# Attention's modulation products dealt out over three projections, shift columns formed later, and a gating accumulator with the tokens innermost

## The chip, the cores and the metric

The kernel runs on one core of one Trainium2 chip. The metric is the device time of one execution in microseconds. Before the change it is 1385.32 us, the median of three runs (1384.69 to 1388.82).

## The reference

Two transformer blocks follow each other on 256 tokens of 1024 channels, all in float32. Both are steered by a conditioning vector: `mod = silu(c) @ ada_w + ada_b` gives six vectors of 1024, a shift, a scale and a gate for each half of the block. What matters here, shortened:

```python
# block 1
sh1, sc1, g1, sh2, sc2, g2 = split(silu(c) @ ada_w + ada_b, 6)
z  = modulate(rms_norm(x), sh1, sc1) @ w_in + b_in      # mLSTM q k v o i f, attention q k v, gates ga gb
ym = mlstm(...) ; ya = attention(rope(q), rope(k), v)   # 256 keys, causal
merged = sigmoid(ga) * (ym @ p_mlstm) + sigmoid(gb) * (ya @ p_moba)
x  = x + g1 * (merged @ w_out)
h  = modulate(rms_norm(x), sh2, sc2)                    # h * (1 + scale) + shift
x  = x + g2 * ((silu(h @ w_gate) * (h @ w_up)) @ w_down)
# block 2: pooling and SSD mixer, then PEER: 8 heads x 16 of 16384 one-neuron experts
act = gelu(h . expert_down[idx]) ; y = sum(gates * act * expert_up[idx])
```

The expert part is computed densely. All 16384 products of a token with `expert_down` are formed and passed through gelu. They are multiplied by a gating matrix that is zero except at a token's 128 chosen experts, and then multiplied with all of `expert_up`.

## The kernel before, in words

Tokens lie along the free dimension and channels along the 128 partitions. Each weight slab is 128 x 1024 float32, 512 KB. The helper `prep` loads it with a DMA from the SP queue (line 210) and splits it into a high part (`hi`, ScalarE, line 213) and a remainder (`lo`, VectorE, line 218). The activations are split in the same way, and each product is made of three matmuls (`mm3`, lines 275 to 279). `prep` runs at most two slabs ahead; there are three buffers each for `hi` and `lo`. TensorE writes into eight PSUM banks: three of the pool `pp` for projections, five of the pool `sp` for everything else.

A modulation vector is not made by TensorE. A column of 128 values is one product on VectorE: `do_ada` (line 228) multiplies a 128 x 1024 slab of `ada_w` by the row `silu(c)` and sums along the row (line 232); a second small instruction reads the accumulator. Eight such products make one of the six vectors, and after the eighth the bias is added (line 240).

The order of the slabs is a list, `items` (lines 156 to 192). `w_items` puts the slabs of one projection on the list, and the products it is given behind particular slabs: `mix` is spread evenly from slab `lo` to the end, `at` names the slabs. `nxt` takes the next weight slab and first runs the products listed ahead of it (`ada_run`). In the first block the projections come in this order: eight double slabs `wst` for the mLSTM, then `win` with 28 slabs (0 to 7 attention's q and k, 8 to 11 its v, 12 to 27 the two gates ga and gb), `pmo` with 8 (merge), `wout` with 8 (output), `wgu` with 44 and `wdn` with 22 (feed-forward).

Work that isn't a projection is written as generators and advanced by `tick` between projections: the mLSTM (lines 555 to 625) during q and k, attention (`moba`, lines 662 to 721) during the gates. Attention's scores are lines 676 and 679 into `sp` banks; VectorE takes row maxima (683, 684); ScalarE takes exponentials and row sums (688); VectorE normalizes (699); TensorE transposes (708 to 710) and multiplies with v. From gate 9 on, the gate projections leave PSUM through a sigmoid (line 752), which needs another table on ScalarE; that table is loaded (lines 94 and 746) after all exponentials before it.

The text's order is not the engines' order. The context is built with `schedule_with_timeline_sim=True`, and each engine's order is fixed when the program is built. In the trace many instructions stand earlier or later than in the text: gate projections run ahead of the attention scores, whose text comes between them.

`residual` (lines 350 to 385) closes a half block, three times in the kernel: for `wout`, for `wdn` and for the second block's `wout2`. For each of eight blocks of 128 channels it runs the projection, adds the gated result to `xT` (366), and stores the scaled `xT` split into `dH` and `dL` (367, 368), with a running sum of squares. The next projection starts before the normalization is known; so `dH` and `dL` have two more columns that hold the shift, formed ahead of the loop (354 to 356), and the projection of a column is scaled and shifted afterwards.

The gating matrix is built in `gstage` (lines 1226 to 1249) for half of the experts at a time, in 32 groups of eight tokens: `gstage(0)` while `expert_down` is multiplied (`dblock`, from 797 us), `gstage(1)` during the first half of `expert_up` (from 1014 us; `umm`, line 1361). A group has one-hot tiles A and B on VectorE (1232 to 1240), 16 matmuls of 64 columns in float16 (1244), which put the eight tokens' 64 columns side by side in one PSUM bank, and a multiplication of the bank into `W` (1248). `W` is stored expert by expert with the 256 tokens innermost, so this multiplication steps through it with the expert innermost, 1 KB from element to element. `wsplit` (1251 to 1267) splits four experts' columns of `W` into high and low part for the expert sum.

Of the kernel before, what the change touches and what calls it, by code (L numbers as in the profile page):

```python
# [9 lines left out]
F32 = mybir.dt.float32  # L10
# [5 lines left out]
AF = mybir.ActivationFunctionType  # L16
OP = mybir.AluOpType
# [3 lines left out]
T = 256  # L21
# [8 lines left out]
GSC = 32768.0  # L30
# [31 lines left out]
def two_block_kernel(ctx, tc, I, out, dbg=None):  # L62
    nc = tc.nc
    V, S, G, PE = nc.vector, nc.scalar, nc.gpsimd, nc.tensor
# [47 lines left out]
    def pp():  # L112
        return ppool.tile([P, 512], F32, name="pp")

    def sp():
        return spool.tile([P, 512], F32, name="sp")
# [41 lines left out]
    def ada_list(w, ms, kind="g"):  # L158
        return [(kind[(i * KD + k) % len(kind)], I["ada%d" % w][m, k], (w, m, k)) for i, m in enumerate(ms) for k in range(KD)]

    def w_items(name, n, mix=(), lo=0, at=None):
        at = at or {}
        for j, a in enumerate(mix):
            at.setdefault(lo + (j * (n - lo)) // len(mix), []).append(a)
        for i in range(n):
            items.append(("w", I[name][i], None))
            items.extend(at.get(i, []))
# [10 lines left out]
        items.append(("w", I["wst"][k], None))  # L178
        items.append(("w", I["wst"][8 + k], None))
    items.append(("c", None, None))  # L180
    attn = ada_list(1, [2, 3, 4], "d")
    w_items("win", 28, attn[:22], 11)
    w_items("pmo", 8, attn[22:])
    w_items("wout", 8)
    ffn = ada_list(1, [5], "d") + [("c", None, None)] + ada_list(2, [0, 1, 2, 3, 4], "d")
    w_items("wgu", 44, ffn[3:30], 12, {6: ffn[:1], 8: ffn[1:2], 10: ffn[2:3]})
    w_items("wdn", 22, ffn[30:])
# [83 lines left out]
    def mcol(w, m, k):  # L271
        o = (w - 1) * 48 + m * 8 + k
        return mod[:, o:o + 1]
# [23 lines left out]
    def paced(ins, to="lo"):  # L297
        after(ins, cur[to])
        return ins
# [24 lines left out]
    def square(src, scale=None):  # L324
        sq = smallp.tile([P, T], F32, name="sq", bufs=3)
        if scale is None:
            S.activation(sq, src, AF.Square)
        else:
            S.activation(sq, src, AF.Square, scale=scale)
        return sq  # L330
# [19 lines left out]
    def residual(emit, w, m, gi, wsh, msh, dH, dL, scale=None, plain=False, post=None, wait=2):  # L350
        acc = smallp.tile([P, T], F32, name="acc", bufs=1)
        accp = smallp.tile([P, T], F32, name="accp", bufs=1) if plain else None
        o_ = sp()
        sh = mod[:, (wsh - 1) * 48 + msh * 8:][:, :8].unsqueeze(2).to_broadcast([P, KD, 2])
        S.activation(dH[:, :, T:], sh, AF.Copy)
        V.tensor_tensor(dL[:, :, T:], sh, dH[:, :, T:].bitcast(F32), OP.subtract)
        for e in range(8):
            ps = cur["ob"][e] if e in cur.get("ob", {}) else sp() if post is not None and e in (3, 4) else pp()
            emit(ps, e)
            g = gs[:, gi, e:e + 1]  # L360
            src = ps[:, :T]
            if post is not None:
                src = smallp.tile([P, T], F32, name="mt", bufs=3)
                V.tensor_tensor(src, ps[:, :T], post, OP.mult)
                V.tensor_tensor(src, src, ps[:, T:], OP.add)
            V.scalar_tensor_tensor(xT[:, e], src, mcol(w, m, e), xT[:, e], OP.mult, OP.add)
            S.activation(dH[:, e, :T], xT[:, e], AF.Copy, scale=g)
            V.scalar_tensor_tensor(dL[:, e, :T], xT[:, e], g, dH[:, e, :T].bitcast(F32), OP.mult, OP.subtract)
            sq = square(xT[:, e], None if scale is None else scale[:, e:e + 1])
            if e == 0:  # L370
                V.tensor_copy(acc, sq)
            elif e < 7:
                V.tensor_tensor(acc, acc, sq, OP.add)
            else:
                PE.matmul(o_[:, :T], ones, acc, start=True, stop=False)
                lag["mm"] = PE.matmul(o_[:, :T], ones, sq, start=False, stop=True)
                lag["wait"] = wait
            if plain:
                sq = square(xT[:, e])
                if e == 0:  # L380
                    V.tensor_copy(accp, sq)
                else:
                    V.tensor_tensor(accp, accp, sq, OP.add)
        cur["h"] = (dH, dL, TE)
        return o_, accp
# [10 lines left out]
    with p1:  # L396
# [245 lines left out]
        for i in range(8):  # L642
            ps = pp()
# [99 lines left out]
        for n in range(16):  # L743
# [5 lines left out]
            ps = pp()  # L749
# [15 lines left out]
        for e in range(8):  # L765
            ps = pp()
# [15 lines left out]
        flush()  # L782
        make_gs(1, 1, 4, "n2")
        o2, _ = residual(lambda ps, e: proj(ps), 1, 2, 1, 1, 3, hH, hL)
        r2 = rstd_of(o2[:, :T], D, "rstd")

    silu_set()
    with ExitStack() as p2:
# [15 lines left out]
        def prescaled(ps, rstd, name, pool):  # L804
            t = pool.tile([P, T], F32, name=name)
            c = pool.tile([P, 1], F32, name=name + "c")
            V.tensor_copy(c, ps[:, T:T + 1])
            V.tensor_tensor(t, ps[:, :T], rstd, OP.mult)
            return t, c

        for f in range(NF):
# [6 lines left out]
            if f < 4:  # L818
                t, c = prescaled(pg, r2, "tg", w2)
                act(s_, t, AF.Silu, bias=c)  # L820
                t, c = prescaled(pu, r2, "tu", w2)
# [35 lines left out]
    with ExitStack() as p3:  # L857
# [147 lines left out]
        pv = q3.tile([P, 4, T], F32, name="pv")  # L1005
# [15 lines left out]
        for g in range(2):  # L1021
            ps = sp()
# [23 lines left out]
        for i in range(8):  # L1046
            ps = pp()
# [48 lines left out]
    W = [wp.tile([P, 64, T], F32, name="W0"), None]  # L1096
# [11 lines left out]
    with ExitStack() as p4:  # L1108
# [86 lines left out]
        for i in range(16):  # L1195
            ps = pp()
# [29 lines left out]
    GT = 8  # L1226

    def gstage(hf):
        for g0 in range(0, T, GT):
            tsl = slice(g0, g0 + GT)  # L1230
            A = q5.tile([P, GT, 64, 2], F16, name="A")
            paced(V.tensor_tensor(A, iob.rearrange("p (n d) -> p n d", d=2)[:, None].to_broadcast([P, GT, 64, 2]),
                                  i1d[:, tsl, None, :].to_broadcast([P, GT, 64, 2]), OP.is_equal))
            yield
            B = q5.tile([P, 2, GT, 32, 2], F16, name="B")
            V.tensor_tensor(B[:, 0], iob[:, hf * 64:hf * 64 + 64].rearrange("p (n d) -> p n d", d=2)[:, None]
                            .to_broadcast([P, GT, 32, 2]), i2d[:, tsl, None, :].to_broadcast([P, GT, 32, 2]), OP.is_equal)
            for j in (1, 0):
                V.tensor_tensor(B[:, j], B[:, 0], gd[j][:, tsl, None, :].to_broadcast([P, GT, 32, 2]), OP.mult)
            yield  # L1240
            ps = pp()
            for t in range(GT):
                for j in range(2):
                    PE.matmul(ps[:, t * 64:(t + 1) * 64], A[:, t].rearrange("p n d -> p (n d)"),  # L1244
                              B[:, j, t].rearrange("p n d -> p (n d)"), start=(j == 0), stop=(j == 1))
            yield
            wv = W[hf][:, :, tsl].rearrange("p n t -> p t n")
            V.scalar_tensor_tensor(wv, ps.rearrange("p (t n) -> p t n", t=GT), 1.0 / GSC, wv, OP.mult, OP.mult)  # L1248
            yield

    def wsplit(n2):
# [314 lines left out]
```

## Time and profile before

| | |
|---|---|
| median of three runs | 1385.32 us |
| the profiled execution | 1386.68 us |
| its span, first to last instruction | 1384.9 us |
| mean granted TensorE clock | 0.993 |
| TensorE busy | 1355.2 us, 98% |
| VectorE busy | 1163.3 us, 84% |
| ScalarE busy | 715.2 us, 52% |
| SP queue | 283.64 MB, 59.1% of 16 DMA engines |

The profile is that of one execution. PE is TensorE's matmuls, PEld its weight loads, DVE is VectorE, ACT is ScalarE, POOL is GpSimd, SP the queue that issues the DMAs. A row by stretch gives, for each engine, its busy time and the count of its instructions in the stretch; then the clock that TensorE was granted as a share of full speed, the DMA engines' share and GB/s. In a row of the waits, the arrow points to what ended the wait. In a timeline row the bracket holds the idle time of the engine ahead of it and what ended it. Rows that follow each other with the same shape are merged, and xN counts them. Matmuls overlap in the pipeline, so their durations are longer than their spacing.

### The profile page before, as it was taken

How to read it: one execution, taken by the hardware profiler on the slowest of the kernel's cores; microseconds unless marked ns; L12 is line 12 of the kernel's file. 1: busy time of each engine (PE TensorE's matmuls, PEld its weight loads, DVE VectorE, ACT ScalarE, POOL GpSimd, SP SyncE). 2: the span in 40 equal slices, each digit the busy share in tenths (PEclk: the TensorE clock that was granted, in tenths of full speed). 3: DMA queues.
4: the chain of work that ended last, by engine and by line, in shares of the span. 5: the costliest groups of instructions: out<-in, count | busy, mean ns of one | idle time of the engine just before them, and what ended most of it. 6: DMA issues, size and time to landing. Idle time of an engine off the chain costs nothing. (4 is left out here: it accounts for less than half of the span.)

```text
span 1384.9 us, 25895 instructions
## 1 busy us (share of the span) xinstructions
PE 1355.2 (98%) x10306; PEld 1254.4 (91%) x10306; DVE 1163.3 (84%) x2015; ACT 715.2 (52%) x1078; POOL 45.9 (3%) x39
## 2 busy tenths in 40 slices
PE   8999899999999999999999999999999999899997
PEld 6998699999999989999999999999978888788886
DVE  7999867988898798788988888888699999776556
ACT  4564665554546946555545544444544444445444
POOL 0000000000000000122222000000000000000000
PEclk9999899999999999999999999999999999999999
DMA  9968645799995435555555544444455555566563
GB/s 339 345 218 298 228 145 176 239 354 346 328 336 207 150 126 173 175 182 183 182 177 170 189 163 161 169 165 168 168 182 178 173 168 170 179 220 221 203 221 107
DMA packets 79196, 286.78 MB, mean 207 GB/s; under 512 B 8817, under 2 KB 9217, under 8 KB 78946
## 3 DMA queue, kind: packets, MB, share of 16 engines
q1 hardware_dynamic: 78770, 283.64, 59.1%
q8 instruction: 81, 1.33, 0.4%
q0 software_dynamic: 304, 1.47, 0.3%
q14 instruction: 41, 0.34, 0.1%
HBM read 284.03 MB, written 1.05 MB: 206 GB/s over the span
## 5 line engine op out<-in xcount | busy, mean ns | idle before, releaser
L213 ACT ACTIVATE hi<-raw 128x1024 fp32r<-128x1024 f32 x382 | 404.9, 1061 | 503.8 <-PE pp L277 236.5
L218 DVE TENSOR_TENSOR lo<-raw,hi 128x1024 fp32r<-128x1024 f32 x366 | 446.4, 1221 | 113.8 <-ACT hi L213 112.9
L278 PE MATMUL pp<-nH,lo 128*128 128x256 f32 x1064 | 300.2, 284 | 2.5 <-DVE lo L218 2.4
L276 PE MATMUL pp<-nH,hi 128*128 128x256 f32 x1064 | 300.3, 284 | 0.3 <-ACT qT L1204 0.3
L277 PE MATMUL pp<-nL,hi 128*128 128x256 f32 x1064 | 300.3, 283 | 0.0
L1361 PE MATMUL sp<-hi,wHL 128*128 128x512 f32 x992 | 257.3, 396 | 3.5 <-ACT wHL L1262 3.5
L276 PE MATMUL pp<-hH,hi 128*128 128x256 f32 (+1 forms) x824 | 236.6, 287 | 0.0
L278 PE MATMUL pp<-hH,lo 128*128 128x256 f32 (+1 forms) x824 | 232.8, 284 | 0.0
L277 PE MATMUL pp<-hL,hi 128*128 128x256 f32 (+1 forms) x824 | 232.8, 283 | 0.0
L1361 PEld LDWEIGHTS sp<-hi,wHL 128*128 128x128 f32 x992 | 185.6, 189 | 44.4 <-ACT wHL L1262 3.9
L278 PEld LDWEIGHTS pp<-nH,lo 128*128 128x128 f32 x1064 | 200.5, 189 | 3.1 <-DVE lo L218 3.1
L276 PEld LDWEIGHTS pp<-nH,hi 128*128 128x128 f32 x1064 | 200.4, 189 | 0.7 <-ACT qT L1204 0.5
L277 PEld LDWEIGHTS pp<-nL,hi 128*128 128x128 f32 x1064 | 200.7, 189 | 0.2
L277 PEld LDWEIGHTS pp<-hL,hi 128*128 128x128 f32 x824 | 156.4, 190 | 1.2 <-issue 1.1
L276 PEld LDWEIGHTS pp<-hH,hi 128*128 128x128 f32 x824 | 156.3, 190 | 0.8 <-issue 0.5
L278 PEld LDWEIGHTS pp<-hH,lo 128*128 128x128 f32 x824 | 156.1, 190 | 0.8 <-issue 0.7
L1361 PE MATMUL sp<-lo,wHL 128*128 128x512 f32 x496 | 136.6, 393 | 0.0
L1361 PEld LDWEIGHTS sp<-lo,wHL 128*128 128x128 f32 x496 | 93.3, 188 | 20.8
L1248 DVE SCALAR_TENSOR_TENSOR W<-pp,W 128x512 f32<-128x512 f32 x64 | 85.3, 1333 | 23.2 <-PE pp L1244 23.2
L213 ACT ACTIVATE hi<-ada 128x1024 fp32r<-128x1024 f32 x52 | 55.2, 1062 | 58.1 <-PE pp L277 29.3
L232 DVE SCALAR_TENSOR_TENSOR raw<-raw,crow 128x1024 f32<-128x1024 f32 x56 | 68.2, 1219 | 5.3 <-DMA raw<-in_ada 5.2
L218 DVE TENSOR_TENSOR lo<-ada,hi 128x1024 fp32r<-128x1024 f32 x52 | 63.5, 1222 | 7.5 <-ACT hi L213 7.0
(464 smaller groups left out, 1984.2 us busy)
## 6 DMA issues: line engine op xcount, KB each, us to landing
raw<-in_edn SPq DMA_DIRECT2D x128, 512.0 KB, 3.3
raw<-in_eup SPq DMA_DIRECT2D x128, 512.0 KB, 4.0
raw<-in_ada SPq DMA_DIRECT2D x64, 512.0 KB, 5.2
raw<-in_win SPq DMA_DIRECT2D x35, 512.0 KB, 4.5
ada<-in_ada SPq DMA_DIRECT2D x32, 512.0 KB, 5.3
raw<-in_wgu SPq DMA_DIRECT2D x32, 512.0 KB, 5.1
ada<-in_win SPq DMA_DIRECT2D x17, 512.0 KB, 4.7
raw<-in_wq SPq DMA_DIRECT2D x15, 512.0 KB, 3.5
```

Of the source, the lines that this page charges most:

```text
L213: cur["hi"] = S.activation(hi, raw, AF.Copy)
L218: cur["lo"] = V.tensor_tensor(lo, raw, hi.bitcast(F32), OP.subtract)
L232: V.scalar_tensor_tensor(raw, raw, 1.0, cur["crow%d" % w], OP.mult, OP.mult, accum_out=mod[:, o:o + 1])
L276: m = PE.matmul(ps, lh, rh, start=start, stop=False)
L277: PE.matmul(ps, lh, rl, start=False, stop=False)
L278: PE.matmul(ps, ll, rh, start=False, stop=stop)
L1248: V.scalar_tensor_tensor(wv, ps.rearrange("p (t n) -> p t n", t=GT), 1.0 / GSC, wv, OP.mult, OP.mult)
L1361: m = PE.matmul(oacc[q], l[:, a * P:(a + 1) * P], u[:, b], start=n2 == 0 and i == 0, stop=n2 == 127 and i == 2, skip_group_check=True)
```

## The change

Three edits.

1. The 24 products for the vectors 2 (gate g1), 3 (shift sh2) and 4 (scale sc2) change their order and their places. Before: 22 spread over `win` slabs 11 to 27, two in `pmo`, none in `wout`. After: the vectors come in the order 2, 4, 3; three products follow `win` slabs 5, 7 and 9, thirteen are spread over slabs 11 to 27, three stand in `pmo`, and the last five, all of the shift, behind the first five slabs of `wout`.
2. `residual` forms the shift columns ahead of the seventh block (`e == 6`) in place of ahead of the loop, in all three uses.
3. `gstage` writes its matmuls' results with the token innermost: the 64 columns of token t go to every eighth element of the bank, from t on. The multiplication then reads the bank in storage order and steps through `W` in runs of eight tokens.

```diff
@@ the list of slabs
-    attn = ada_list(1, [2, 3, 4], "d")
-    w_items("win", 28, attn[:22], 11)
-    w_items("pmo", 8, attn[22:])
-    w_items("wout", 8)
+    attn = ada_list(1, [2, 4, 3], "d")
+    w_items("win", 28, attn[3:16], 11, {5: attn[:1], 7: attn[1:2], 9: attn[2:3]})
+    w_items("pmo", 8, attn[16:19])
+    w_items("wout", 8, (), 0, {j: attn[19 + j:20 + j] for j in range(5)})
@@ residual
-        S.activation(dH[:, :, T:], sh, AF.Copy)
-        V.tensor_tensor(dL[:, :, T:], sh, dH[:, :, T:].bitcast(F32), OP.subtract)
         for e in range(8):
+            if e == 6:
+                S.activation(dH[:, :, T:], sh, AF.Copy)
+                V.tensor_tensor(dL[:, :, T:], sh, dH[:, :, T:].bitcast(F32), OP.subtract)
@@ gstage
             ps = pp()
+            pv = ps.rearrange("p (n t) -> p n t", t=GT)
             for t in range(GT):
                 for j in range(2):
-                    PE.matmul(ps[:, t * 64:(t + 1) * 64], A[:, t].rearrange("p n d -> p (n d)"),
+                    PE.matmul(pv[:, :, t], A[:, t].rearrange("p n d -> p (n d)"),
                               B[:, j, t].rearrange("p n d -> p (n d)"), start=(j == 0), stop=(j == 1))
             yield
-            wv = W[hf][:, :, tsl].rearrange("p n t -> p t n")
-            V.scalar_tensor_tensor(wv, ps.rearrange("p (t n) -> p t n", t=GT), 1.0 / GSC, wv, OP.mult, OP.mult)
+            wv = W[hf][:, :, tsl]
+            V.scalar_tensor_tensor(wv, pv, 1.0 / GSC, wv, OP.mult, OP.mult)
             yield
```

## Rows read from the trace of the kernel before

**Rows 1.** The page, part 1: busy us (share) xinstructions of each engine.

```profile
PE 1355.2 (98%) x10306; PEld 1254.4 (91%) x10306; DVE 1163.3 (84%) x2015; ACT 715.2 (52%) x1078; POOL 45.9 (3%) x39
```

**Rows 2.** By stretch, end of the input projection: length, busy us (count), clock, DMA.

```profile
156.70:161.20 4.50, 0.42 (x2) 0.19 (x1) 4.50 (x12) 1.02 (x4) 0.00 (x0) 0.88 0.58 223
161.20:168.60 7.40, 5.05 (x15) 3.65 (x16) 2.76 (x14) 6.47 (x29) 0.00 (x0) 0.50 0.39 143
168.60:173.60 5.00, 4.99 (x24) 4.98 (x25) 5.00 (x20) 4.99 (x14) 0.00 (x0) 0.50 0.00 0
173.60:190.00 16.40, 16.40 (x140) 14.65 (x140) 8.51 (x15) 12.43 (x24) 0.00 (x0) 0.99 0.34 107
```

**Rows 3.** Waits of TensorE after 96 us: total us, times, longest us.

```profile
PE sp L676 <- DVE ada L232: 4.1, 1, 4.1
PE sp L1361 <- ACT wHL L1262: 3.5, 1, 3.5
...
PE sp L708 <- DVE P L699: 2.3, 1, 2.3
```

**Rows 4.** VectorE's instructions in order: start us, us, line, operation, tiles, shapes.

```profile
149.05 0.69 DVE L640 TENSOR_TENSOR ro<-ro,rot 128x512 f32<-128x512 f32 x1
...
156.04 1.28 DVE L683 TENSOR_REDUCE nm<-sp 128x2 f32<-128x512 f32 x2
157.24 1.22 DVE L232 SCALAR_TENSOR_TENSOR raw<-raw,crow 128x1024 f32<-128x1024 f32 x1
...
159.98 1.22 DVE L232 SCALAR_TENSOR_TENSOR ada<-ada,crow 128x1024 f32<-128x1024 f32 x1
```

**Rows 5.** ScalarE's instructions in order, the softmax.

```profile
160.17 0.47 ACT L107 ACTIVATE P<-sp,nm 128x256 f32<-128x256 f32 x1 [5.46 <-DVE nm L684]
...
167.87 1.28 ACT L94 ACT_TABLE_LOAD   x1
```

**Rows 6.** By stretch, input to output projection.

```profile
55.00:88.00 33.00, 33.00 (x260) 31.70 (x259) 28.60 (x54) 24.38 (x47) 0.00 (x0) 1.00 0.66 248
88.00:161.00 73.00, 69.12 (x466) 59.64 (x464) 68.88 (x107) 36.49 (x59) 0.00 (x0) 0.99 0.82 294
161.00:215.00 54.00, 51.44 (x387) 48.29 (x388) 36.46 (x80) 36.01 (x86) 0.00 (x0) 0.88 0.39 137
215.00:240.00 25.00, 24.56 (x202) 24.23 (x201) 18.61 (x33) 15.35 (x28) 0.00 (x0) 1.00 0.51 169
```

**Rows 7.** Line 232 from 88 to 161 us: count, then duration ns min/median/max.

```profile
L232 DVE SCALAR_TENSOR_TENSOR raw<-raw,crow x14: 1214/1216/1219, 90.7 to 157.2; 128x1024 f32<-128x1024 f32 x14
...
L232 DVE SCALAR_TENSOR_TENSOR ada<-ada,crow x9: 1214/1217/1220, 88.5 to 160.0; 128x1024 f32<-128x1024 f32 x9
```

**Rows 8.** By stretch, VectorE at line 232 alone.

```profile
88.00:161.00 73.00, 27.87 (x45) 0.99 0.82 294
```

**Rows 9.** By stretch, the second gating half, before its last multiplications.

```profile
1000.00:1188.00 188.00, 188.00 (x1228) 152.36 (x1227) 177.80 (x235) 80.05 (x77) 0.00 (x0) 1.00 0.52 174
```

**Rows 10.** VectorE's instructions in order, the last gating multiplication.

```profile
1191.21 1.15 DVE L1248 SCALAR_TENSOR_TENSOR W<-pp,W 128x512 f32<-128x512 f32 x1
```

**Rows 11.** ScalarE's instructions in order, start of the second half.

```profile
1191.83 1.06 ACT L107 ACTIVATE W<-W 128x1024 f32<-128x1024 f32 x1 [1.92 <-DMA W<-in_cr]
...
1192.99 1.99 ACT L1262 ACTIVATE wHL<-W 128x1024 fp32r<-128x1024 f32 x2
```

**Rows 12.** TensorE's instructions in order, start of the second half.

```profile
1194.09 3.57 PE L1361 MATMUL sp<-hi,wHL 128*128 128x512 f32 x8 [3.52 <-ACT wHL L1262]
...
1198.52 1.98 PE L1361 MATMUL sp<-hi,wHL 128*128 128x512 f32 x8
```

**Rows 13.** The page, part 5: xcount | busy us, mean ns | idle.

```profile
L1248 DVE SCALAR_TENSOR_TENSOR W<-pp,W 128x512 f32<-128x512 f32 x64 | 85.3, 1333 | 23.2 <-PE pp L1244 23.2
```

**Rows 14.** Groups of VectorE by line, 120 to 160 us.

```profile
L639 DVE TENSOR_TENSOR rot<-sp,sin_t 128x512 f32<-128x512 f32 x3 | 2.1, 684 | 1.5 <-PE sp L636 1.5
```

**Rows 15.** By stretch, TensorE at line 1244 alone.

```profile
1188.92:1189.87 0.95, 0.95 (x32) 0.95 (x32) 1.00 1.06 392
```

## The prediction

> **What bounds the kernel now.** I read the engine line of the page first. TensorE is busy 1355.2 of 1384.9 us [rows 1], so a change that adds no matmul can win back only TensorE's idle time and the time it runs at a low clock. The views by stretch and by wait then say where these are. Three places matter here.
>
> The first is the end of the input projection. From 156.7 to 168.6 us TensorE is busy only 5.5 of 11.9 us, so 6.4 us are idle; and from 161.2 to 173.6 its granted clock is 0.50, that is 1.2 of 2.4 GHz, after the idle stretch before it. The busy time at that level is 5.05 + 4.99 = 10.0 us, of which half, 5.0 us, would not be needed at full clock [rows 2]. Together 11.4 us. The waits name the scores' matmuls (line 676, 4.1 us) and the transposes of the softmax (line 708, 2.3 us), both held by VectorE [rows 3]. The reader should see how: the last rope sum ends at 149.7, the row maxima of the first scores start only at 156.0, and between and after them VectorE runs two modulation products, at 157.24 and 159.98 [rows 4]. ScalarE's first exponential waits for the scaled maximum until 160.17 [rows 5], and a PSUM bank for the next scores comes free only after it. The sigmoid table follows the last exponential at 167.87 [rows 5], so the gate projections that have to leave PSUM through a sigmoid wait too. Nothing was left for TensorE to run beside this chain.
>
> The second is the cause of that lateness: VectorE is busy 68.9 of 73 us from 88 to 161 [rows 6], and 23 products of 1.21 us, with their accumulator reads 27.87 us, run there [rows 7, 8].
>
> The third is the start of the second half of the expert sum. VectorE is busy 177.8 of 188 us before it [rows 9]; the last gating multiplication starts at 1191.21 [rows 10], ScalarE's split of the gated weights at 1192.99 [rows 11], and TensorE waits 3.5 us for it [rows 3] and then runs slowly: eight matmuls take 3.57 us where the next such eight take 1.98 [rows 12]. That place costs 3.5 + 1.6 = 5.1 us.
>
> **Part 1: products dealt out.** Before, all 24 attention products but one run by 161. After, three follow input slabs 5, 7 and 9 (counted from 0), thirteen slabs 11 to 27, three stand in the merge projection and five in the output projection. No product and no DMA is added or removed: 24 slabs of 512 KB stay on the SP queue, only later in it. From 88 to 161 VectorE gets 13 products for 23: 10 x 1.21 = 12.1 us less on 68.9. Three of the ten go ahead of 88, where VectorE has 33 - 28.6 = 4.4 us free for 3.6 us [rows 6]. The other seven go behind 161.
>
> What is that worth? If the maxima follow the scores directly, the two products inside the first wait go (2.4 us of the 4.1). If the ropes and the normalizer chain of the mLSTM, which share VectorE, end some 10 us earlier, the scores come up while several gate projections of some 2.8 us (24 matmuls; 140 in 16.4 us in the stretch at 0.99 of full clock [rows 2]) are still to run, and these cover the softmax chain, whose length is set by ScalarE from 160.17 to 167.87 [rows 5]. So the gain lies between 2.4 us and all 11.4 us; below nothing I exclude for this term alone, since the chain only gets shorter. I take 7.5 us: both the idle time and the low clock shrink together, because the clock falls only behind the idle time, but some exposed chain will stay.
>
> The price is behind 161. From 161 to 215 VectorE has 54 - 36.5 = 17.5 us free, and takes two products more. From 215 to 240, the output projection, it has 25 - 18.6 = 6.4 us free and takes five, 6.1 us [rows 6]. TensorE runs 24.56 of 25 us there. What waits behind a product on VectorE is the next slab's low part and the residual sum that frees a PSUM bank; TensorE is up to three banks ahead, so a delay of one or two products is absorbed, one of all five (6.1 us) is not. Bounds: 0 and 6.1 us. I take 0.5 us, because part of the free time lies at the stretch's start, before the first block's result is there, and the products need only their DMA.
>
> **Part 2: shift columns late.** Three pairs of instructions on 16 columns, a copy on ScalarE and a subtraction on VectorE, move behind the sixth of eight blocks. Before, the pair could stand early because the shift products were done; now the first pair waits for the last product. Behind it in the queues are the seventh block's scale and split. The readers are the first feed-forward matmuls, which need the eighth block as well. Cost 0; if the last product were late it would be a part of the 6.1 us above, not a new term.
>
> **Part 3: interleaved gating accumulator.** 1024 matmuls of 64 columns write every eighth fp32 of a bank in place of 64 neighbours, and 64 multiplications read the bank straight and walk the weights in runs of eight neighbours in place of steps of 1 KB. The multiplication takes 1333 ns now [rows 13]; a VectorE operation on as many elements, also with one operand in PSUM but neighbours in SBUF, takes 684 [rows 14]. Bounds for it: 1333 to 684, so 0 to 64 x 0.65 = 42 us of VectorE, nearly all of it beside TensorE's work. On the path lies only the third place, at most 5.1 us. Since the ScalarE operation before the split waits for a row that a DMA lands at 1191.83 [rows 11], a faster multiplication alone wins next to nothing there; the order of the instructions would have to come out better too. I take 2 us.
>
> The matmuls' own price is not shown by any row of the trace. Now 32 of them take 0.95 us, 29.7 ns each [rows 15], so TensorE spends 30.4 us on all 1024. Below, a write to scattered addresses costs what one to neighbours costs: 0. Above, I take VectorE's ratio for scattered addresses, 1333 / 684 = 1.95, as the nearest row: 1024 x 29.7 x 0.95 = 29 us, all on the path, since TensorE is the bound in both gating stretches. I take 0: that ratio belongs to another engine and another memory, and to steps of 1 KB, not of 32 bytes. But both ends stay in the range.
>
> [...]
>
> **The sum.** The profiled execution took 1386.68 us, 1.8 over its span of 1384.9 and 1.4 over the median of 1385.32. From it: -7.5 (softmax chain) + 0.5 (output projection) + 0 (shift columns) - 2 (gating tail) + 0 (scattered writes) = -9, or 1377.7. Against the median: 1376.3. I say 1377. The likeliest case's own range: its bounds are -11.4 - 5.1 = -16.5 and -2.4 + 0 + 6.1 = +3.7; with terms seldom all at one end, 1370 to 1383.
>
> **Rivals.**
> - *Scattered PSUM writes at half rate.* +29 us on the 1024 matmuls, while the other terms stay; with TensorE slower, VectorE has time to finish the gating, so the third place's 5.1 us go whole. 1385.3 + 29 - 7 - 5 = 1402. If only the second matmul of each pair, which adds to what is there, pays: 1388. For it: VectorE's 1.95 on scattered addresses in SBUF, and TensorE already at one column in 0.46 ns, so no slack hides it. Against it: nothing was measured in PSUM. It decides the sign from a spacing of about 29.7 + 9000 / 1024 = 38.5 ns upward. Chance 0.28; slower.
> - *The order stays.* The scores stand in TensorE's order behind most gate projections because of where they are set when the program is built; if they stay there, VectorE's free time is of no use before them, and only the two products within the wait go: -2.4 and some low clock, 1382 to 1385. For it: the projections of later text already stand ahead of the scores now. Against: they stand there because VectorE brings the ropes late, and this is what is relieved. Chance 0.16; mostly no measurable change.
> - *The output projection becomes the new bound.* Five products of 1.21 us into 6.4 us free: the residual sums come late, TensorE runs out of banks, and up to 6 us and some low clock take the place of what the softmax gave back: 1385. For it: VectorE's free time there equals the added work. Against: the merge stretch ahead has 17.5 us free. Chance 0.06; no change or a little slower.
> - The forecast: chance 0.50.
>
> A difference under 0.3% (4.2 us) can't be told from none by such a measurement. The forecast gives faster for nearly all of its 0.50, a little of it no change; with a share of the second rival, faster 0.50. No change: the rest of the second and third, and of the forecast: 0.20. Slower: the first rival and the tails, 0.30. The range must reach over both sides: 1369 to 1404.
>
> **What would show it.** Right: the granted clock stays at 1.00 through the softmax, the scores' matmuls stand between gate projections, the wait of line 676 is under 1 us, the multiplication (line 1248, 1250 in the changed file) takes about 0.7 us, 32 gating matmuls still take 0.95 us, and TensorE stays busy through the output projection. Wrong: 32 gating matmuls take 1.9 us (first rival); TensorE still idles behind line 676 with no projection left (second); TensorE waits for a low part or a bank in the output projection (third).

## The result, and the profile after

The changed kernel takes 1405.39 us (median of four, 1404.21 to 1407.31) beside 1385.61 us for the kernel before: a ratio of 1.014, 95% interval 1.012 to 1.016. It is some 20 us slower, where 8 us faster were forecast, and 1.4 us above the end of the range. The profiled execution took 1404.21 us, its span is 1402.3, 17.4 more than before.

The page's engine line answers to [rows 1].

```profile
PE 1377.2 (98%) x10306; PEld 1277.2 (91%) x10306; DVE 1126.6 (80%) x2015; ACT 715.6 (51%) x1078; POOL 46.7 (3%) x39
```

TensorE has the same 10306 matmuls and is busy 22.0 us longer; VectorE is busy 36.7 us less. So the time is not idle time: the matmuls themselves became dearer. Where, four points of the timeline show.

| | before | after | stretch up to here |
|---|---|---|---|
| ones-matmuls at the end of the first half block | 238.37 | 233.99 | -4.4 |
| first gating matmul | 796.86 | 792.66 | +0.2 |
| first matmul of the expert sum | 996.2 | 1003.3 | +11.3 |
| last matmul of the expert sum | 1376.9 | 1394.1 | +10.1 |
| end of the span | 1384.9 | 1402.3 | +0.2 |

The two stretches that lost are those with the gating matmuls. The same 32 matmuls as in [rows 15], TensorE at the gating line alone:

```profile
1208.11:1209.88 1.77, 1.77 (x32) 1.77 (x32) 1.00 1.01 329
```

1.77 us for 32 is 55.3 ns each, against 29.7. Over all 1024 the starts lie 54.9 ns apart on average (29.7 before), 25.9 us more in sum; the spacing is 56 ns after the first matmul of a pair and after the second, which adds to the first, alike. What the edit bought is on VectorE, the page's costliest groups, against [rows 13]:

```profile
L1250 DVE SCALAR_TENSOR_TENSOR W<-pp,W 128x512 f32<-128x512 f32 x64 | 44.1, 690 | 49.1 <-PE pp L1246 49.1
```

The multiplication is down from 1333 to 690 ns, 41 us in all, and TensorE spent 21.4 us more in the two stretches. The end of the input projection, by stretch, with the start of the output projection as the last row (columns as in [rows 2]):

```profile
150.00:160.00 10.00, 8.29 (x55) 6.56 (x53) 8.52 (x21) 5.61 (x24) 0.00 (x0) 1.00 0.31 100
160.00:170.00 10.00, 7.35 (x43) 7.11 (x45) 8.00 (x27) 9.64 (x30) 0.00 (x0) 0.66 0.26 99
170.00:180.00 10.00, 10.00 (x89) 8.95 (x86) 4.74 (x7) 7.59 (x17) 0.00 (x0) 1.00 0.46 159
...
210.00:220.00 10.00, 8.72 (x67) 8.14 (x68) 9.50 (x20) 5.89 (x12) 0.00 (x0) 1.00 0.73 264
```

From 150 to 170 TensorE is idle 4.4 us, where it was 6.4 [rows 2], and its clock is low for a part of ten microseconds (a mean of 0.66) in place of 12.4 at 0.50; if all of it was at 0.50 or at 1.00, that is some 6.8 us. From 210 to 220 it is idle 1.3 us. Of the waits behind that, one of 0.44 us stood in the kernel before too, after 215 (24.56 us busy of 25 in [rows 6]), so some 0.9 us are new. VectorE's queue shows what still holds the chain, against [rows 4]:

```profile
150.50 1.28 DVE L684 TENSOR_REDUCE nm<-sp 128x2 f32<-128x512 f32 x2
152.98 1.23 DVE L232 SCALAR_TENSOR_TENSOR ada<-ada,crow 128x1024 f32<-128x1024 f32 x1 [1.20 <-DMA ada<-in_ada]
...
154.13 0.23 DVE L685 TENSOR_SCALAR nm<-nm 128x2 f32<-128x2 f32 x2
```

and ScalarE's first exponential and table load, against [rows 5]:

```profile
154.39 0.48 ACT L107 ACTIVATE P<-sp,nm 128x256 f32<-128x256 f32 x1 [4.54 <-DVE nm L685]
...
161.91 1.28 ACT L94 ACT_TABLE_LOAD   x1
```

The scores start at 148.3 (153.1 before) and their maxima at 150.5. Then VectorE stands idle 1.2 us for the DMA of a modulation slab and makes that product, and only behind it comes the small scaling that the first exponential waits for. The exponentials up to the table take 7.5 us (7.7 before), the table's load 1.28 us as before. TensorE's waits, against [rows 3]:

```profile
PE sp L709 <- DVE P L700: 3.4, 1, 3.4
PE sp L1363 <- ACT wHL L1264: 1.4, 1, 1.4
...
PE pp L276 <- ACT hi L213: 1.0, 2, 0.6
PE sp L677 <- ACT P L107: 1.0, 2, 0.8
```

The scores' own wait (line 676 before, 677 now) is down from 4.1 to 1.0 us, that for the normalized weights has grown from 2.3 to 3.4 us, and the one at the second half of the expert sum is 1.4 in place of 3.5. The two waits for ScalarE's high part (line 276) are in the output projection, one of them the 0.44 us from before. That place in TensorE's timeline, against [rows 12]:

```profile
1208.11 1.96 PE L1246 MATMUL pp<-B,A 128*128 128x64 f16 x32
...
1212.01 1.20 PE L1363 MATMUL sp<-hi,wHL 128*128 128x512 f32 x4 [1.41 <-ACT wHL L1264]
1213.78 1.19 PE L1363 MATMUL sp<-hi,wHL 128*128 128x512 f32 x4 [0.58 <-DVE wHL L1265]
```

The last gating matmuls stand where they stood, directly ahead of the matmuls that need their result. Eight of these now take 2.97 us from 1212.01 to their end, for 3.57; the granted clock is 1.00 here (1205 to 1220) and was 0.54 before (1194.09 to 1197.78). By stretch, against [rows 6]:

```profile
55.00:88.00 33.00, 33.00 (x263) 31.81 (x262) 30.27 (x58) 24.08 (x45) 0.00 (x0) 1.00 0.75 264
88.00:161.00 73.00, 70.29 (x475) 60.79 (x473) 62.16 (x102) 41.64 (x82) 0.00 (x0) 1.00 0.70 242
161.00:215.00 54.00, 52.00 (x416) 49.86 (x416) 41.32 (x83) 32.03 (x64) 0.00 (x0) 0.94 0.55 192
215.00:240.00 25.00, 23.95 (x193) 23.47 (x194) 21.55 (x41) 18.89 (x33) 0.00 (x0) 1.00 0.61 205
```

### The profile page after: what moved, and what is told of

The parts are those of the page before. It is cut to its first block, busy times and chain, and to the rows that moved or that the text cites. A ratio compares the mean times of both kernels' runs of the same rounds, so it can differ in the third digit from the quotient of the medians.

```text
span 1402.3 us, 25880 instructions
## 1 busy us (share of the span) xinstructions
PE 1377.2 (98%) x10306; PEld 1277.2 (91%) x10306; DVE 1126.6 (80%) x2015; ACT 715.6 (51%) x1078; POOL 46.7 (3%) x39
## 3 DMA queue, kind: packets, MB, share of 16 engines
HBM read 284.03 MB, written 1.05 MB: 203 GB/s over the span
## 4 chain that ended last, share of the span: by engine, by line
PE 93%; DVE 3%; DMA 1%; ACT 1%; issue 1%; SPq 0%; DVEq 0%; ACTq 0%
PE sp L1363 25%; PE pp L276 18%; PE pp L278 18%; PE pp L277 18%; PE pp L1246 4%; DVE lo L218 1%; DMA ada<-in_ada 1%; ACT hi L213 1%; PE sp L1127 1%; PE pp L1087 0%; DMA ada<-in_wst 0%; PE pp L1088 0%; PE pp L1086 0%; ACT P L107 0%; PE sp L457 0%
## 5 line engine op out<-in xcount | busy, mean ns | idle before, releaser
L1250 DVE SCALAR_TENSOR_TENSOR W<-pp,W 128x512 f32<-128x512 f32 x64 | 44.1, 690 | 49.1 <-PE pp L1246 49.1
```

Source lines behind the costliest of these rows:

```text
L1250: V.scalar_tensor_tensor(wv, pv, 1.0 / GSC, wv, OP.mult, OP.mult)
```

## The experiments

The theory: a matmul that writes single fp32 elements with a step into PSUM takes nearly twice as long (55.3 ns for 29.7 in these two profiles); this alone turned the sign, while dealing out the products is a gain of 4 us. The rival: the gating matmuls were slowed by the new order, or the gain of dealing out isn't its own. Each ratio below is to executions of the kernel before made in the same set; there were three sets, with medians of 1387.14, 1388.76 and 1387.49 us for that kernel. A gain in us is worked out from the ratio.

**Part 3 alone.** The diff is the third edit of the change, on the kernel before.

> The kernel before with part 3 alone (gating results written with the token innermost; products and shift columns as before). Theory A: a TensorE matmul that writes every eighth fp32 of a PSUM bank takes 54.9 ns in place of 29.7, whatever else runs; 1024 x 25.3 = 26 us more, less 1 to 2 us at the start of the second half of the expert sum, where the faster multiplication shortens TensorE's wait: 1385.5 + 24 to 25 = 1409 to 1411 us, and VectorE's multiplication at 0.69 us. Rival: the matmuls were slowed by what the dealt-out products did to the order and the timing; then the spacing here stays near 30 ns and the time is 1383 to 1386.

Measured 1410.98 us: 1.0169 (95% interval 1.0155 to 1.0183), 23.4 us slower. Sixteen matmuls of one group, and VectorE's multiplication:

```profile
862.72:863.59 0.87, 0.87 (x16) 0.87 (x16) 1.00 0.44 66
```

```profile
L1249 DVE SCALAR_TENSOR_TENSOR W<-pp,W 128x512 f32<-128x512 f32 x64 | 44.0, 688 | 49.1 <-PE pp L1245 49.1
```

0.87 us for 16, the mean spacing over all is 54.9 ns. The matmuls are as dear without the dealt-out products; the rival falls.

**Parts 1 and 2 alone.** The diff is the first two edits.

> The kernel before with parts 1 and 2 alone (products dealt out, shift columns late; gating written and multiplied as before). Theory A: in the changed kernel the first half block ends 4.4 us earlier than before (the ones-matmuls at 233.99 for 238.37 us), and nothing later gives it back: 1381.2 us, faster by 0.3%. Rival: the 4.4 us came with the changed gating order or are lost again at a wait behind (feed-forward, second block): 1384 to 1386.

Measured 1384.85 us: 0.9979 (0.9967 to 0.999), 2.9 us faster, between the theory (1381.2 of 1385.61 is 0.9968) and the rival (0.9988 and up), neither of which the interval clearly excludes. With part 3 alone it makes 1.0148, and the change has 1.014 (1.012 to 1.016): the parts add. The profile has the end of the half block at 235.0 (238.37 before) and TensorE's waits as follows, then the same wait for tile A in the kernel before:

```profile
PE sp L1362 <- ACT wHL L1263: 4.0, 1, 4.0
PE sp L709 <- DVE P L700: 3.4, 1, 3.4
PE pp L1245 <- DVE A L1233: 1.8, 3, 0.6
```

```profile
PE pp L1244 <- DVE A L1232: 1.8, 3, 0.6
```

The gating still waits as in the kernel before, 1.8 us for tile A and 4.0 us (3.5 before) at the second half; the softmax's wait is that of the changed kernel. So the two edits act in different stages.

**Runs of two.** The gating results are written so that two experts of a token lie side by side; VectorE then needs two multiplications of 256 elements:

```diff
-            pv = ps.rearrange("p (n t) -> p n t", t=GT)
+            pw = ps.rearrange("p (m t d) -> p t m d", t=GT, d=2)
-                    PE.matmul(pv[:, :, t], A[:, t].rearrange("p n d -> p (n d)"),
-                              B[:, j, t].rearrange("p n d -> p (n d)"), start=(j == 0), stop=(j == 1))
+                    PE.matmul(pw[:, t], A[:, t].rearrange("p n d -> p (n d)"),
+                              B[:, j, t], start=(j == 0), stop=(j == 1))
...
+            for d in range(2):
+                wv = W[hf][:, :, tsl].rearrange("p (m d) t -> p d m t", d=2)[:, d]
+                V.scalar_tensor_tensor(wv, pw[:, :, :, d].rearrange("p t m -> p m t"), 1.0 / GSC, wv, OP.mult, OP.mult)
```

> Parts 1 and 2, and the gating results written in runs of two neighbours: experts 2m and 2m+1 of one token lie side by side, the next pair follows 16 elements on. VectorE multiplies in two instructions of 256 elements. [...] Theory A2 (any output pattern with a step pays, or the price goes by the distance): spacing 43 to 55 ns, time 1395 to 1406.

Measured 1380.58 us: 0.9956 (0.9943 to 0.997).

```profile
849.02:849.50 0.48, 0.48 (x16) 0.48 (x16) 1.00 0.00 0
```

```profile
L1251 DVE SCALAR_TENSOR_TENSOR W<-pp,W 128x256 f32<-128x256 f32 x128 | 48.1, 417 | 31.7 <-PE pp L1246 31.5
```

16 matmuls take 0.48 us, 30 ns each, where theory A2 had 43 to 55: the price is gone, though the pairs lie 64 bytes apart. So in these runs it is not a step as such that costs, but an element without a neighbour (54.9 ns for 30).

**A step of two.** The converse: two tokens interleaved, so that no element has a neighbour but the next one is only 8 bytes away.

```diff
+            p2 = ps.rearrange("p (h n u) -> p h n u", h=GT // 2, u=2)
-                    PE.matmul(pv[:, :, t], A[:, t].rearrange("p n d -> p (n d)"),
+                    PE.matmul(p2[:, t // 2, :, t % 2], A[:, t].rearrange("p n d -> p (n d)"),
...
+            for h in range(GT // 2):
+                wv = W[hf][:, :, g0 + 2 * h:g0 + 2 * h + 2]
+                V.scalar_tensor_tensor(wv, p2[:, h], 1.0 / GSC, wv, OP.mult, OP.mult)
```

> Parts 1 and 2, and the gating results of two tokens interleaved (a step of two fp32, 8 bytes, in place of eight); VectorE multiplies in four instructions of 128 elements. Theory A1 (two neighbours are needed, the distance doesn't matter): spacing 55 to 56 ns as with a step of eight. Theory A3 (the price grows with the distance): between 30 and 50 ns.

One run, without an interval: 1406.26 us, and the spacing

```profile
854.71:855.58 0.87, 0.87 (x16) 0.87 (x16) 1.00 0.31 89
```

is 0.87 us for 16, 54 ns each, as with a step of eight (0.87 us in part 3 alone). At 8 bytes the price is the same as at 32, so between these two the distance does not matter. The two runs together: a matmul of 64 columns takes 30 ns where each element has a neighbour and 54 ns where it has none. Whether a pair has to begin at an even element was not tried.

**Reading with a step.** TensorE writes as before, VectorE reads the bank with a step and still walks the weights in runs of eight:

```diff
-            wv = W[hf][:, :, tsl].rearrange("p n t -> p t n")
-            V.scalar_tensor_tensor(wv, ps.rearrange("p (t n) -> p t n", t=GT), 1.0 / GSC, wv, OP.mult, OP.mult)
+            wv = W[hf][:, :, tsl]
+            V.scalar_tensor_tensor(wv, ps.rearrange("p (t n) -> p n t", t=GT), 1.0 / GSC, wv, OP.mult, OP.mult)
```

> Parts 1 and 2; TensorE writes the eight tokens' 64 columns side by side as before, and VectorE reads the bank with a step of 64 elements, so that it still walks the weights in runs of eight tokens. Theory A: spacing 29.7 ns; what the multiplication takes tells which memory made it slow before: 0.69 us if it was the step of 1 KB in SBUF, about 1.33 us if scattered addresses in PSUM are as dear to VectorE. Time 1379 to 1381 in the first case (the tail before the second half of the expert sum is shorter), 1381 to 1382 in the second. Rival: none faster than the dealt-out products alone.

Measured 1378.13 us: 0.9939 (0.9926 to 0.9953), 8.5 us faster than before. This is faster than both kernels. The matmuls (32 of them), VectorE's multiplication, and two of TensorE's waits:

```profile
1179.77:1180.71 0.94, 0.94 (x32) 0.94 (x32) 1.00 0.99 353
```

```profile
L1249 DVE SCALAR_TENSOR_TENSOR W<-pp,W 128x512 f32<-128x512 f32 x64 | 43.9, 687 | 32.1 <-PE pp L1245 32.1
```

```profile
PE sp L709 <- DVE P L700: 3.4, 1, 3.4
PE sp L1362 <- ACT wHL L1263: 1.9, 1, 1.9
```

VectorE takes 687 ns, with a PSUM step of 64 elements. So the 1333 ns came from the step of 1 KB in SBUF, and a step in PSUM costs VectorE nothing that shows (687 ns, and 688 in storage order in part 3 alone). TensorE pays nothing either (0.94 us for 32 matmuls, 0.95 before). From the first gating matmul to the expert sum it takes 197.4 us (199.3 before), and the expert sum 378.3 (380.7): VectorE's 41 us are worth some 4 us.

**The same on the kernel before**, without the dealt-out products.

> The kernel before (products and shift columns untouched) with VectorE reading the bank with a step of 64 elements and walking the weights in runs of eight tokens. Theory: the gain of this edit and that of dealing out add, as they lie in different stages: together 0.9939, dealt out alone 0.9979, so this alone about 0.996, 1381 to 1383 us for a before of 1387; the waits of the gating matmuls for VectorE in the first half (1.8 us) go, and TensorE's wait at the start of the second half falls from 3.5 to about 2 us. Rival: without the dealt-out products it gives nothing.

Measured 1382.86 us: 0.9974 (0.9963 to 0.9984), 3.6 us faster; the first half takes 197.4 us again and the wait at the second is shorter:

```profile
PE sp L1361 <- ACT wHL L1262: 2.3, 1, 2.3
```

3.6 and 2.9 us alone, 8.5 together: the two add, within the intervals.

**Part 2 alone.** The diff is the second edit, the shift columns formed at expert column 6.

> The kernel before with part 2 alone, the shift columns formed ahead of the seventh block in all three uses. Theory: no effect, within 0.3% of before; the ends of the half blocks within what two executions of one program differ by. Rival: the copy or the subtraction stands ahead of the seventh block's scale and delays the end of a half block by up to 1 us.

Measured 0.9999 (0.9985 to 1.0012). No effect, and the softmax's waits are those of the kernel before:

```profile
PE sp L677 <- DVE ada L232: 4.1, 1, 4.1
PE sp L709 <- DVE P L700: 2.3, 1, 2.3
```

**No products at all.** The 24 products and their loads are left out, so the three vectors are zero.

```diff
-    attn = ada_list(1, [2, 3, 4], "d")
-    w_items("win", 28, attn[:22], 11)
-    w_items("pmo", 8, attn[22:])
+    V.memset(mod, 0.0)
+    w_items("win", 28)
+    w_items("pmo", 8)
```

> The kernel before without attention's 24 modulation products and without the loads of their slabs; the three vectors are left zero, so the values that follow are not the reference's. It bounds what dealing them out could give. Theory A (VectorE's load and the products that stand between maxima and scaling hold the softmax chain, all 11.4 us of it): the first half block ends 9 to 11 us earlier than before, 1375 to 1377 us. Theory B (most of the exposed chain is set by its own dependences and by the order of the instructions, not by products): it ends 5 to 7 us earlier, 1379 to 1381, and TensorE still waits some 3 us for the normalized weights.

Measured 1377.97 us: 0.9918 (0.9899 to 0.9938). The half block ends at 228.5, 9.9 us earlier than before, as the first theory had it. By stretch:

```profile
88.00:161.00 73.00, 73.00 (x486) 61.81 (x485) 49.07 (x86) 46.19 (x98) 0.00 (x0) 1.00 0.38 123
161.00:215.00 54.00, 54.00 (x456) 53.13 (x456) 38.64 (x62) 33.91 (x58) 0.00 (x0) 1.00 0.50 162
215.00:240.00 25.00, 25.00 (x208) 24.89 (x207) 21.18 (x41) 17.80 (x30) 0.00 (x0) 1.00 0.57 177
```

TensorE is busy all the time from 88 to 240 at full clock; the scores start at 131.2 and the softmax chain runs wholly beside projections. The order on TensorE shows how. When the scores start, 289 matmuls of the gate projections are still to come (24 to a slab), and 97 of them, four slabs, stand between the scores and the softmax's first transpose. In the kernel before these counts are 96 and 0, in the changed kernel 121 and 25. So the 11.4 us were to be had, but dealing out brought only one slab beside the chain, and 2.9 us over the whole kernel. What is left hangs on the products that stay or on their loads; this run takes out both.

**Products out of the softmax's way.** On the fastest version, no product behind input slabs 19 to 27:

```diff
-    w_items("win", 28, attn[3:16], 11, {5: attn[:1], 7: attn[1:2], 9: attn[2:3]})
-    w_items("pmo", 8, attn[16:19])
+    w_items("win", 28, (), 0, {**{5: attn[:1], 7: attn[1:2], 9: attn[2:3]},
+                                **{j: attn[j - 8:j - 7] for j in range(11, 19)}})
+    w_items("pmo", 8, attn[11:19])
```

> The same version, but the products of input slabs 19 to 27 moved on: three behind slabs 5, 7, 9, eight behind slabs 11 to 18, eight in the merge projection, five in the output projection. In the changed kernel a product stands on VectorE between the first maxima and their scaling, and waits there for its DMA; here none does. Theory A: the first exponential comes some 2 us earlier against the scores' matmuls, and the first half block ends 2 us earlier. Rival: eight products in the merge projection keep VectorE full there, TensorE waits for low parts, and the 2 us are given back.

Measured 0.9947 (0.9934 to 0.9961), not told apart from 0.9939 and not the gain expected. Half of the theory held: the first exponential

```profile
154.90 0.47 ACT L107 ACTIVATE P<-sp,nm 128x256 f32<-128x256 f32 x1 [2.09 <-DVE nm L685]
```

comes 3.6 us after the scores' first matmul, where it was 5.9. But the scores started later in this execution, at 151.3 for 147.2, and behind them:

```profile
160.00:170.00 10.00, 6.22 (x34) 5.78 (x34) 8.47 (x27) 8.79 (x27) 0.00 (x0) 0.68 0.61 210
...
200.00:215.00 15.00, 14.09 (x116) 13.68 (x115) 15.00 (x25) 5.43 (x8) 0.00 (x0) 1.00 0.85 292
215.00:240.00 25.00, 23.91 (x190) 23.12 (x191) 22.25 (x42) 15.57 (x28) 0.00 (x0) 1.00 0.70 244
```

VectorE is full from 200 to 215 and TensorE loses 0.9 us there and 1.1 at the output projection, together 2.0, for 1.4 in the fastest version; the 0.6 more is spent waiting for low parts, as the rival has it. But the 2.3 us of the first exponential were given back earlier, at the softmax's end. VectorE there:

```profile
162.68 1.23 DVE L232 SCALAR_TENSOR_TENSOR ada<-ada,crow 128x1024 f32<-128x1024 f32 x1
...
163.83 1.22 DVE L218 TENSOR_TENSOR lo<-raw,hi 128x1024 fp32r<-128x1024 f32 x1
164.97 0.25 DVE L694 RECIPROCAL rc<-sm 128x16 f32<-128x16 f32 x1
```

A product and a low part now stand ahead of the reciprocal of the row sums, and the first transpose comes 14.3 us after the scores' first matmul, as in the fastest version (14.2).

**No products in the output projection**, on the fastest version.

```diff
-    w_items("pmo", 8, attn[16:19])
-    w_items("wout", 8, (), 0, {j: attn[19 + j:20 + j] for j in range(5)})
+    w_items("pmo", 8, attn[16:24])
+    w_items("wout", 8)
```

> The same version, but no product in the output projection: sixteen in the input projection as in the changed kernel and eight in the merge projection. In the changed kernel TensorE loses 1.3 us from 210 to 220, at the start of the output projection. Theory A: that is the price of the five products there; the loss goes and the half block ends 1 us earlier. Rival: the products' time only moves, VectorE is late by as much at the same place, and the half block ends at the same time or later.

Measured 0.9957 (0.9942 to 0.9972), no gain. The products of the merge projection were pulled ahead, into the softmax:

```profile
154.68 1.23 DVE L232 SCALAR_TENSOR_TENSOR ada<-ada,crow 128x1024 f32<-128x1024 f32 x1 [1.39 <-DMA ada<-in_ada]
...
163.93 1.23 DVE L232 SCALAR_TENSOR_TENSOR raw<-raw,crow 128x1024 f32<-128x1024 f32 x1 [1.61 <-DMA raw<-in_ada]
...
165.08 0.25 DVE L694 RECIPROCAL rc<-sm 128x16 f32<-128x16 f32 x1
```

A second product now stands, after a wait for its DMA, directly ahead of the reciprocal that all normalization needs. In the changed kernel TensorE waits three times in and just ahead of the output projection, 0.35 us for a low part of VectorE and 0.61 and 0.44 us for high parts of ScalarE. Here the first is gone and the other two stand, 1.05 us from 215 to 240. So the five products account for some 0.35 us; 0.44 us stood in the kernel before, and what brings the 0.61 stays open.

**The second gating half started earlier**, at expert column 2 for 4, on the fastest version.

```diff
-        if n2 == 4:
+        if n2 == 2:
             gens.append(gstage(1))
```

> The version with dealt-out products, results written side by side and read with a step, and the second gating half started two expert columns earlier (2 for 4). Theory A: TensorE's wait at the start of the second half of the expert sum is due to where the last two gating groups stand in TensorE's order; started 5.6 us earlier, the wait of 1.9 us and the low clock after it go: 2 to 4 us less than the same version without it. Rival: the groups' order is set by VectorE's load as the order was planned, the last two groups stand at the same place, and nothing changes.

Measured 0.9941 (0.9926 to 0.9955), no gain; the rival was right. TensorE's timeline:

```profile
1179.82 1.11 PE L1245 MATMUL pp<-B,A 128*128 128x64 f16 x32
1184.09 2.15 PE L1362 MATMUL sp<-hi,wHL 128*128 128x512 f32 x6 [3.17 <-ACT wHL L1263]
```

The 32 last gating matmuls stand again directly ahead of the matmuls that need them. Their place comes from the order as it was planned, not from where the text starts them.

**Half of the late products on GpSimd and ScalarE**, on the fastest version.

```diff
+    attn[3:16] = [("g" if i % 2 else "d",) + a[1:] for i, a in enumerate(attn[3:16])]
```

> Dealt-out products and stepped reading, and six of the thirteen products of input slabs 11 to 27 made by GpSimd (the multiplication) and ScalarE (the sum along the row) in place of VectorE. Without any product the first half block ended 9.9 us earlier than before, dealt out 4 to 6. Theory A (VectorE's time is what the softmax chain waits for): 7 us less of VectorE between 88 and 161 brings the half block's end 2 to 4 us earlier, 0.992. [...]

Measured 0.9964 (0.995 to 0.9977), no gain, and rather slower than the version it was put on (0.9939, 0.9926 to 0.9953). The scores do start 8.7 us earlier, at 138.5, with 200 gate matmuls still to come for 121. But the exponentials gain less. In order: ScalarE, VectorE, GpSimd:

```profile
146.53 1.06 ACT L239 ACTIVATE raw<-raw 128x1024 f32<-128x1024 f32 x1 [6.04 <-POOL raw L235]
...
147.59 0.45 ACT L107 ACTIVATE P<-sp,nm 128x256 f32<-128x256 f32 x1
```

```profile
144.28 2.31 DVE L686 TENSOR_SCALAR nm<-nm 128x2 f32<-128x2 f32 x2
```

```profile
144.14 2.36 POOL L235 TENSOR_TENSOR raw<-raw,crow 128x1024 f32<-128x1024 f32 x1 [10.30 <-DMA raw<-in_ada]
```

ScalarE's row sum stands ahead of the first exponential and waits 6.0 us for GpSimd's multiplication, whose slab's DMA was late. An operation in the middle of the chain was moved to another engine, where it again stood ahead of it.

Nor did VectorE get free time: from 88 to 161 it is busy 60.9 us here and 61.4 in the version without GpSimd, with 92 instructions for 103. Line 525, three of whose 24 operations ran beside GpSimd's multiplications, shows why (count, then duration in ns, min/median/max):

```profile
L525 DVE SCALAR_TENSOR_TENSOR acc<-zp,prm,acc x24: 464/476/2631, 60.5 to 112.3; 128x256 f32<-128x256 f32 x24
```

Beside five of the six multiplications one VectorE operation took 2.2 to 3.1 us in place of 0.2 to 1.2 and ended only after GpSimd had. That is some 10 us, more than the 7.3 us of the six products that VectorE gave up. So GpSimd's multiplications cost VectorE time; by what way, no run shows.

## Why the prediction was wrong

The step that failed is the price of the gating matmuls: "I take 0: that ratio belongs to another engine and another memory, and to steps of 1 KB, not of 32 bytes." The chip's answer is 25.9 us for the 1024 matmuls, 54.9 ns each for 29.7, and part 3 alone made the kernel 23.4 us slower. The first rival had the mechanism, at a chance of 0.28. That its 29 us came so near was luck: they are VectorE's ratio for a step of 1 KB in SBUF, and the same engine paid nothing for a step in PSUM (687 ns beside 690). Its 1402 us came near because the price was 3 us too high and the gains beside it too, 7 and 5 us where parts 1 and 2 alone gave 2.9 and the faster multiplication alone 3.6.

Of the reasons for 0, another engine and another memory was true, but where no row bears on a matmul's scattered write it is a reason to weigh both ends, not to take the lower one. The size of the step was no reason: steps of 8 and of 32 bytes cost the same (0.87 us for 16 matmuls), and pairs 64 bytes apart cost nothing (0.48 us). The prediction's own remark that at 0.46 ns a column no slack would hide a price pointed the right way.

Of the signs it named, the multiplication took its 0.7 us, and the scores' wait came down to 1.0 us. The 32 gating matmuls took 1.77 us, near the first rival's 1.9; the clock did not stay at 1.00 through the softmax (0.66 from 160 to 170), and TensorE did not stay busy through the output projection (23.95 of 25 us).

The other terms, in their order:

- Softmax chain, -7.5 taken, bounds 2.4 to 11.4. Counted as the prediction counts, the idle time fell from 6.4 to 4.4 us and the loss to the low clock from 5.0 to some 2.5 (an estimate: of the 6.8 us at that level TensorE was busy some 4.9). So the term is about -4.5. The level of 0.50, put in the prediction as 1.2 of 2.4 GHz, shows in the spacing: in the kernel before, matmuls of 256 columns lie 213 ns apart there (170 to 173.6 us), 1.2 columns a ns or, over 0.50, 2.4; at 1.00 they lie 119 ns apart (median), 2.15 columns a ns, so that for these a little less than half of the busy time is lost. With the next term in it, the half block's end moved by -4.4, and parts 1 and 2 alone gave 2.9 us over the whole kernel. The cause was right: without any product, the whole chain hides. The size was off because "several gate projections" were to cover the chain and one did: 25 matmuls stand between the scores and the first transpose, where there were none, and without products there are 97. VectorE's load from 88 to 161 fell by 6.7 us (68.9 to 62.2) and not by 12.1.
- Output projection, +0.5 taken. TensorE is idle 1.3 us at its start, some 0.9 of it new, within the bounds; the five products account for about 0.35 of it, by the run without them.
- Shift columns, 0: right, 0.9999.
- Gating tail, -2 taken, bounds 0 to 5.1. Within the bounds: beside the matmuls' 12.9 us in each half, the stretches grew by 11.3 and 10.1, so VectorE's faster multiplication gave 1.6 and 2.8 us (an estimate that has the matmuls' whole price on TensorE's path). The 1.6 in the first half, where gating matmuls had waited for VectorE, weren't in the sum. The reading experiment, which has this without the price, gives 3.6 us alone. The prediction held that a faster multiplication alone would win next to nothing at the third place; in that experiment the wait there fell from 3.5 to 2.3 us by it alone.

Of the other rivals, "the order stays" was nearly right for parts 1 and 2: the scores came 4.8 us earlier, but with only one slab more of the gates left behind them (121 matmuls for 96), and the 1384.85 us of these parts alone lie in its 1382 to 1385. "The output projection becomes the new bound" was not borne out, with 0.9 us new there. One caution on the profiles: the first half block of kernels that are alike up to there ends between 237.5 and 241.3 us (before, part 3 alone, part 2 alone, reading alone) and between 232.1 and 235.4 in the six profiles with the change's dealing, so single profiles place it to 2 us.

## What to carry to other kernels

When a step through memory has to fall somewhere between a matmul and a VectorE operation, let VectorE read PSUM with it; TensorE's write paid for elements without a neighbour (54.9 ns for 29.7), VectorE's read paid nothing (687 ns beside 690). A price that no row shows is to be tried by itself before it is joined to a likely gain: here part 3 alone cost 23.4 us, and parts 1 and 2 alone gave 2.9. And work that is moved off a busy engine helps only if what remains doesn't stand, waiting for its own transfer, between two steps of the chain that was to be freed.

## What the runs showed of the hardware

That a matmul's scattered write costs the same in the first matmul of a pair as in the second, which adds to what is there (56 ns both), was not expected: it is the write, not the adding. That VectorE reads PSUM with a step of 64 elements at the same 687 ns as in storage order (690) was open. And in the last experiment VectorE operations were held up beside GpSimd's multiplications of 128 x 1024 elements, which take 2.4 to 2.9 us. Three of 128 x 256 elements took 2.56 to 2.63 us (median 0.48), a low part 3.07 (1.22), and the 128 x 2 scaling shown above 2.24; each ended after the multiplication beside it. A RECIPROCAL beside the sixth took 1.75 us, as without GpSimd (1.74), so not every operation is held. No run was made to tell which are.
